# w_out with tokens stationary and 512 columns moving, its sum kept by tokens

## The chip, the cores and the metric

The kernel runs on one core of a Trainium2 chip. The metric is the device time of one execution in microseconds (us). The core has a tensor engine (PE, with the weight loads shown apart as PEld), a vector engine (DVE), a scalar engine (ACT), a general engine (POOL) and a queue engine (SP). Each works off its own instructions in order and waits for the others by semaphores. Here SP issues the weight loads.

## The reference

One layer of a backbone is computed for 128 context tokens and 256 latent tokens (384 in all), with D = 2048 features. What matters is the middle of the layer:

```
def trunk_layer(x, mod, p, ...):
    shift1, scale1, gate1, shift2, scale2, gate2 = jnp.split(mod[:, None, :], 6, axis=-1)
    h = rmsnorm(x, p['norm1']) * (1.0 + scale1) + shift1
    y, kv, st = token_mixers(h, p, ...)          # ends with  y @ p['w_out']
    x = x + gate1 * y
    h = rmsnorm(x, p['norm2']) * (1.0 + scale2) + shift2
    x = x + gate2 * conv_ffn(h, p['w_up'], ..., p['w_down'])
    return x, kv, st
```

`mod` is silu(c) @ w_mod + b_mod: six sections of 2048 columns, with one row of conditioning for the context tokens and one for the latent ones. All is float32.

## The kernel before

**Weights.** All weights stream through SBUF once, in chunks of 128 x 1024 values (512 KB). A `Chunk` is loaded by SP into one of six `raw` buffers, in the order of the list `chunks`, up to five chunks ahead (`LD`). A weight chunk is split in two halves (`do_split`): ACT casts to `hi` (L358), DVE subtracts to get `lo` (L359), each with five buffers. Every product is three matmuls: hi x hi, hi x lo, lo x hi. Two forms exist. `add_wstat` holds 128 x 128 weights in PE and moves 384 token columns (L368 to L370; 386 in w_up, which appends two shift columns); its result lies by features. `add_xstat` holds 128 tokens and moves up to 512 weight columns (L425 to L427); its result lies by tokens, in three of the four banks of `mm_bank`.

**Order.** `chunks` is a list written at trace time, in which `mark(f)` puts code to run at that place. `defer(n, f)` puts `f` off by n half chunks, `settle` runs all that is put off, `pump` steps side work (attention, mLSTM, loads) after each half chunk. The engines' own order comes out of a scheduler that takes the instructions by priority (their order in the code) as it expects them to be ready. The buffers of a tag are handed out in code order.

**Late modulation.** The modulation for the first norm is computed by PE. The other columns of w_mod are done by DVE: `by_dve` is a list of 128 chunks, for 16 blocks of 512 columns, 8 chunks each, in the order 8, 16, 12 (group 0), 9, 17, 13 (group 1), 10, 18, 14, 11, 19, 15, and 20, 21, 22, 23 (group 4). Blocks 8 to 11 are gate 1, 12 to 15 shift 2, 16 to 19 scale 2, 20 to 23 gate 2. `late_mod` adds one chunk into `lacc` (a tag with one buffer) with four DVE instructions (L263, L265). After a block's eighth chunk, `late_sum` sums over partitions on PE (L290, 4 half chunks later), and then `late_out` transposes the block into features (L299), or, for gate 2, `late_row` adds the bias on DVE (L280) and writes a row to DRAM from POOL (L283).

`spread(main, share)` takes a stage's chunks and puts a `by_dve` chunk behind them whenever the shares add up to one. `finish_late(b)` puts all that is left of groups up to b at its place. The shares (`dens`) are 0.25, 0.25, 0.75 and 0.8 for the stages before w_out, 0.5 in w_out and in w_up.

**The stages around the change.** `phase_out(i)`, i from 0 to 7, multiplies by 256 columns of w_out with weights stationary. `load_x1` has fetched x by tokens and transposed it into features (L923); `evac_out` adds gate 1 times the product (L940), squares (L933, L935) and, half a chunk later, `scaled` writes the second input `hh` and its rest (L961, L962). `second_scale` sums the squares over partitions by two matmuls with ones (L971, L972). Then come eleven groups of w_up (`add_up`); from the third on, w_down follows every second group in four blocks of 512 columns (`add_down`), tokens stationary. While the first groups of w_up run, `to_tokens` transposes the sum back to tokens (L1025), to which `gated` adds gate 2 times the product (L1039, L1041). Gate 2 comes as a row from DRAM (`add_rows`), spread over all partitions, in a chunk of its own ahead of a block's last chunk.

Of the kernel before, what the change touches and what calls it, by code (L numbers as in the profile page):

```python
# [7 lines left out]
F32 = mybir.dt.float32  # L8
# [6 lines left out]
P = 128  # L15
# [20 lines left out]
def hybrid_step(  # L36
# [212 lines left out]

    late_acc = {}  # L250

# [17 lines left out]

    gate2 = drp.tile([4, 2 * 512], F32, name="gate2", tag="gate2")  # L270

    def late_row(blk, ev):
        b = blk % 4
        br = sp.tile([P, P], F32, name=nm("brow"), tag="ko")
        G.memset(br, 0.0)
        for i in range(4):
            c0 = 512 * blk + 128 * i
            G.dma_start(out=br[32 * i:32 * i + 1], in_=b_mod[0, c0:c0 + 128].rearrange("(o d) -> o d", o=1))
        for j in range(2):
            V.tensor_tensor(ev[:, 128 * j:128 * j + 128], ev[:, 128 * j:128 * j + 128], br, ALU.add)  # L280
        row = gate2[b:b + 1].rearrange("o (j i c) -> o i j c", j=2, i=4)
        for i in range(4):
            G.dma_start(out=row[:, i], in_=ev[32 * i:32 * i + 1].rearrange("p (j c) -> p j c", j=2))  # L283

    def late_sum(blk):
        acc = late_acc.pop(blk)
        ps = sd_bank()
        for i in range(4):
            for j in range(2):
                T.matmul(ps[32 * i:32 * i + 32, 128 * j:128 * j + 128], lhsT=ones[:, 0:32], rhs=acc[:, j, 128 * i:128 * i + 128],  # L290
                         start=True, stop=True, tile_position=(0, 32 * i))
        ev = sp.tile([P, 256], F32, name=nm("lev"), tag="ropa", bufs=3)
        A.copy(ev, ps[:, 0:256])
        defer(3, lambda: (late_row if blk // 4 == 5 else late_out)(blk, ev))

# [37 lines left out]
    class Chunk:  # L333
        def __init__(self, src, shape, mm, split=True, by_rows=True):
            self.src, self.shape, self.mm, self.split, self.by_rows = src, shape, mm, split, by_rows
            self.raw, self.parts = None, []

        def load(self):
            k, ncol = self.shape
            self.raw = rawp.tile([P, CK], F32, name=nm("raw"), tag="raw")  # L340
            self.v = self.raw[:, :k * ncol].rearrange("p (k c) -> p k c", k=k)
            S.dma_start(out=self.v, in_=self.src)
# [558 lines left out]

    x1 = [None] * KT
    sqacc = const([P, NTOK], "sqacc")

    def load_x1():

        got = {}

        def fetch_x(i):
            a, b = XP[i]  # L910
            for t in range(3):
                got[i, t] = xp.tile([P, NX], F32, name=nm("xa"), tag=f"xl{3 * (i % 5) + t}")
                G.dma_start(out=got[i, t][:, :P * (b - a)], in_=xsrc[t][:, P * a:P * b])

        for i in range(5):
            fetch_x(i)
            yield
        for n in range(KT):
            if n == 4:
                fetch_x(5)  # L920
            ps = sd_bank()
            for t in range(3):
                T.transpose(ps[:, 128 * t:128 * t + 128], got[n // 3, t][:, 128 * (n % 3):128 * (n % 3) + 128], ident)  # L923
            if n % 4 == 0:
                x1g = xp.tile([P, 4, NTOK], F32, name=f"x1_{n}", tag=f"xg{n // 4}")
            x1[n] = x1g[:, n % 4]
            A.copy(x1[n], ps[:, :NTOK])
            yield

    def square_sum(n):  # L930

        q = sqacc if n == 0 else sp.tile([P, NTOK], F32, name=nm("sq"), tag="pT", bufs=3)
        A.activation(q, x1[n][:, :NTOK], AF.Square)  # L933
        if 0 < n < KT - 1:
            V.tensor_tensor(sqacc, sqacc, q, ALU.add)  # L935
        return q

    def residual(n, ps, sec):
        for j, (a, b) in enumerate(SEGS):
            V.scalar_tensor_tensor(x1[n][:, a:b], ps[:, a:b], mod[:, sec, n, j:j + 1], x1[n][:, a:b], ALU.mult, ALU.add)  # L940

    def evac_out(n, ps):
        residual(n, ps, 2)
        q = square_sum(n)
        defer(1, lambda: scaled(n))
        if n == KT - 3:

            A.activation(epsc[:, 1:2], sqacc[:, 0:1], AF.Ln, bias=epsc[:, 0:1])
        if n == KT - 1:
            second_scale(q)  # L950

# [3 lines left out]

    def scaled(n):
        h = xp.tile([P, NX], R32, name=f"hh{n}", tag=f"xl{n}")
        l = slot("hl", R32)[:, :NX]
        x2[n] = (h, l)
        for j, (a, b) in enumerate(SEGS):  # L960
            A.activation(h[:, a:b], x1[n][:, a:b], AF.Copy, scale=sc_[:, 1, n, j:j + 1])  # L961
            V.scalar_tensor_tensor(l[:, a:b], x1[n][:, a:b], sc_[:, 1, n, j:j + 1], h[:, a:b].bitcast(F32),  # L962
                                   ALU.mult, ALU.subtract)
        A.copy(h[:, NTOK:NX], mod[:, 3, n])
        V.tensor_tensor(l[:, NTOK:NX], mod[:, 3, n], h[:, NTOK:NX].bitcast(F32), ALU.subtract)

    rtok = {}

    def second_scale(q):
        ps = sd_bank()  # L970
        T.matmul(ps[:, :NTOK], lhsT=ones, rhs=sqacc, start=True, stop=False)  # L971
        T.matmul(ps[:, :NTOK], lhsT=ones, rhs=q, start=False, stop=True)  # L972
        v = sp.tile([P, 2, NTOK], F32, name="rv", tag="E", bufs=2)
        t = sp.tile([P, 2, NTOK], F32, name="rt", tag="E", bufs=2)[:, 0]
        r = rtok["r"] = slot("rtok")[:, :NX]
        V.memset(r[:, NTOK:NX], 1.0)
        A.activation(v[:, 1], ps[:, :NTOK], AF.Ln, bias=epsc[:, 0:1], scale=1.0 / D)
        V.tensor_scalar(v[:, 0], ps[:, :NTOK], 1.0 / D, EPS, ALU.mult, ALU.add)
        A.activation(r[:, :NTOK], v[:, 1], AF.Exp, scale=-0.5)
        V.tensor_tensor(t, r[:, :NTOK], r[:, :NTOK], ALU.mult)  # L980
        V.scalar_tensor_tensor(t, t, -0.5, v[:, 0], ALU.mult, ALU.mult)
        V.scalar_tensor_tensor(r[:, :NTOK], t, 1.5, r[:, :NTOK], ALU.add, ALU.mult)

# [30 lines left out]

    x1t = [None] * 4

    def to_tokens():
        for b in range(4):  # L1020
            two = s2p.tile([P, 2, 512], F32, name=nm("x1s"), tag="sc")
            banks = [two[:, 0], two[:, 1], sd_bank()]
            for i in range(4):
                for t in range(3):
                    T.transpose(banks[t][:, 128 * i:128 * i + 128], x1[4 * b + i][:, 128 * t:128 * t + 128], ident)  # L1025
                yield
            x1t[b] = xp.tile([P, 3, 512], F32, name=f"x1t{b}", tag=f"xg{b}")
            for t in range(3):
                A.copy(x1t[b][:, t], banks[t])
            yield  # L1030

    def add_rows(src, use):

        ch = Chunk(src.to_broadcast([P, CK]).rearrange("p (k c) -> p k c", k=2), (2, 512), use, split=False)
        return ch

    def gated(t, b, c0, n, ps, gate):

        V.tensor_tensor(ps, ps, gate[:, min(t, 1), c0:c0 + n], ALU.mult)  # L1039
        x = x1t[b][:, t, c0:c0 + n]  # L1040
        V.tensor_tensor(x, x, ps, ALU.add)  # L1041

    def add_down(s_, b):
# [3 lines left out]
                  lambda t, ps: gated(t, b, 0, 512, ps, g2["v"]),  # L1047
                  add_rows(gate2[b:b + 1], lambda ch: g2.update(v=ch.v)))

# [38 lines left out]
    def last_tokens(t):  # L1088
        ssq = sp.tile([P, 5], F32, name=nm("ssqf"), tag="sm")
        at = 0  # L1090
        for b, (c0, c1) in enumerate(BL):
# [12 lines left out]
            while at < 5 and 512 * SQ[at][0] + SQ[at][2] <= c1:  # L1104
                q, a, e = SQ[at]
                junk = sp.tile([P, 2, 512], F32, name=nm("junk"), tag="lacc", bufs=1)[:, 0]
                A.activation(junk[:, 0:e - a], x1t[q][:, t, a:e], AF.Square, accum_out=ssq[:, at:at + 1])
                at += 1
# [113 lines left out]

    def phase_out(i):
        add_wstat(w_out[0], KT, 256 * i, lambda k: ys[k], lambda j, ps: evac_out(2 * i + j, ps))

# [7 lines left out]

    def drain():
        while side:
            pump()

    def settle():
# [5 lines left out]
    finish_late(0)  # L1244
    for i in range(8):
        if i % 2 == 0:
            mark(settle)
        spread(taken(phase_out, i), dens[4])
        finish_late(min(3, i // 2 + 1))

# [6 lines left out]
    for g in range(ngr):  # L1257
        if g == 0:
            mark(lambda: side.append(to_tokens()))
        spread(taken(add_up, g), dens[5])  # L1260
        if g == 2:

            finish_late(4)
            mark(settle)
        if g == 2:
            mark(drain)
        if g >= 2 and g % 2 == 0:
# [6 lines left out]
    for b in range(4):  # L1274
        chunks.append(add_rows(gate2[b:b + 1], lambda ch, b=b: fin["g"].update({b: ch.v})))
        if b % 2:
# [95 lines left out]
```

## Time and profile before

| | |
|---|---|
| median of 3 runs | 2288.24 us (2286.62 to 2288.36) |
| the profiled execution | 2288.0 us |
| its span, first to last instruction | 2286.2 us |
| mean granted clock of PE | 0.999 |
| DVE, busy in the span | 1637.4 us |
| ACT, busy in the span | 1028.0 us |
| POOL, busy in the span | 133.0 us |

A row of a group reads: line, engine, operation, output <- inputs, shapes, count | busy time, mean ns of one | idle time of the engine before, and who ended it. A row of the timeline reads: start, duration, engine, line, operation, shapes, count. Times in the timeline are us from the span's start. Matmuls overlap one another, so their durations add up to more than their engine's time.

### The profile page before, as it was taken

The page shows a single profiled execution, that of the slowest core. Times are in us where ns is not written, and L with a number is a line of the kernel's source. Part 1 is how long each engine was busy: PE and PEld are TensorE (multiplying, and loading weights), DVE is VectorE, ACT ScalarE, POOL GpSimd, SP SyncE. Part 2 cuts the span into 40 slices and gives each one's busy share as a digit, 9 for nine tenths or more (in the row PEclk, how much of TensorE's full clock was granted, in tenths as well). Part 3 has the DMA queues.
Part 4 walks back from the last instruction along what each step waited for, and adds up shares of the span by engine and source line. Part 5 has one row for each costly group of instructions (what it writes and reads, how often), then busy time and mean ns, then how long its engine had stood idle before and what let it go on. Part 6 is the DMA issues. An engine that isn't in the chain of part 4 may idle for free.

```text
span 2286.2 us, 35489 instructions
## 1 busy us (share of the span) xinstructions
PE 2247.7 (98%) x13060; PEld 2096.7 (92%) x13060; DVE 1637.4 (72%) x3419; ACT 1028.0 (45%) x2128; POOL 133.0 (6%) x231
## 2 busy tenths in 40 slices
PE   6999999999999999999999999999999999999998
PEld 5888997899999999999999998998999899889987
DVE  5777777767888989878878895555555556555576
ACT  5232355666555433344454542444345345434541
POOL 1000222211110100010000000000000000000000
PEclk9999999999999999999999999999999999999999
DMA  8787644445555667776645555444433444443462
GB/s 269 251 247 243 188 135 124 131 136 148 171 173 171 177 204 234 226 249 189 189 150 179 179 194 157 129 125 134 155 121 124 153 136 123 131 155 122 137 211 84
DMA packets 306990, 386.13 MB, mean 169 GB/s; under 512 B 16709, under 2 KB 231221, under 8 KB 306817
## 3 DMA queue, kind: packets, MB, share of 16 engines
q1 hardware_dynamic: 301168, 375.24, 53.4%
q0 software_dynamic: 4784, 7.06, 1.1%
q8 instruction: 102, 1.67, 0.3%
q10 hardware_dynamic: 864, 1.57, 0.2%
q14 instruction: 72, 0.58, 0.1%
HBM read 379.08 MB, written 4.74 MB: 168 GB/s over the span
## 4 chain that ended last, share of the span: by engine, by line
PE 92%; DMA 3%; DVE 3%; ACT 1%; issue 1%; SPq 0%; POOL 0%; DVEq 0%; ACTq 0%; POOLq 0%
PE mm L368 22%; PE mm L369 22%; PE mm L370 22%; PE mm L425 6%; PE mm L427 6%; PE mm L426 6%; DMA raw<-in_w_mod_dram 1%; PE mb L227 1%; DMA raw<-in_w_in_dram 1%; DVE lo L359 1%; DVE lacc L265 1%; PE mm L1097 1%; PE mm L1096 1%; PE mm L1098 1%; PE sd L826 1%
## 5 line engine op out<-in xcount | busy, mean ns | idle before, releaser
L358 ACT CAST hi<-raw 128x512 fp32r<-128x512 f32 x960 | 590.6, 620 | 984.3 <-PE mm L369 590.9
L359 DVE TENSOR_TENSOR lo<-raw,hi 128x512 fp32r<-128x512 f32 x960 | 659.0, 692 | 477.4 <-ACT hi L358 473.7
L368 PE MATMUL mm<-hh,hi 128*128 128x386 f32 x1408 | 480.1, 341 | 0.0
L369 PE MATMUL mm<-hl,hi 128*128 128x386 f32 x1408 | 479.6, 341 | 0.0
L370 PE MATMUL mm<-hh,lo 128*128 128x386 f32 x1408 | 478.8, 340 | 0.0
L368 PE MATMUL mm<-xg,hi 128*128 128x384 f32 x1024 | 354.4, 347 | 2.2 <-ACT hi L358 1.4
L265 DVE SCALAR_TENSOR_TENSOR lacc<-raw,scT,lacc 128x512 f32<-128x512 f32 x480 | 342.5, 747 | 17.9 <-DMA raw<-in_w_mod_dram 17.7
L369 PE MATMUL mm<-xl,hi 128*128 128x384 f32 x1024 | 345.8, 338 | 0.0
L370 PE MATMUL mm<-xg,lo 128*128 128x384 f32 x1024 | 345.2, 337 | 0.0
L368 PEld LDWEIGHTS mm<-hh,hi 128*128 128x128 f32 x1408 | 267.9, 190 | 1.1 <-ACT hi L358 0.4
L370 PEld LDWEIGHTS mm<-hh,lo 128*128 128x128 f32 x1408 | 266.9, 190 | 0.0
L369 PEld LDWEIGHTS mm<-hl,hi 128*128 128x128 f32 x1408 | 266.5, 189 | 0.3
L368 PEld LDWEIGHTS mm<-xg,hi 128*128 128x128 f32 x1024 | 192.3, 188 | 21.2 <-issue 14.0
L369 PEld LDWEIGHTS mm<-xl,hi 128*128 128x128 f32 x1024 | 192.5, 188 | 1.5 <-issue 1.4
L370 PEld LDWEIGHTS mm<-xg,lo 128*128 128x128 f32 x1024 | 192.3, 188 | 0.4 <-issue 0.2
L427 PE MATMUL mm<-hi,gl 128*128 128x512 f32 x480 | 189.2, 394 | 0.0
L426 PE MATMUL mm<-lo,gh 128*128 128x512 f32 x480 | 189.2, 394 | 0.0
L425 PE MATMUL mm<-hi,gh 128*128 128x512 f32 x480 | 186.8, 394 | 0.0
L425 PEld LDWEIGHTS mm<-hi,gh 128*128 128x128 f32 x480 | 90.2, 188 | 21.3 <-DVE x1t L1041 0.2
L427 PEld LDWEIGHTS mm<-hi,gl 128*128 128x128 f32 x480 | 90.2, 188 | 21.0
L426 PEld LDWEIGHTS mm<-lo,gh 128*128 128x128 f32 x480 | 90.2, 188 | 20.9
L503 DVE TENSOR_TENSOR qk<-qk,mm 128x384 f32<-128x384 f32 x160 | 85.7, 549 | 21.4 <-PE mm L370 20.9
(350 smaller groups left out, 3065.3 us busy)
## 6 DMA issues: line engine op xcount, KB each, us to landing
raw<-in_w_mod_dram SPq DMA_DIRECT2D x192, 512.0 KB, 4.4
raw<-in_w_up_dram SPq DMA_DIRECT2D x176, 512.0 KB, 3.6
raw<-in_w_in_dram SPq DMA_DIRECT2D x160, 512.0 KB, 4.6
raw<-in_w_down_dram SPq DMA_DIRECT2D x80, 512.0 KB, 3.9
raw<-in_w_out_dram SPq DMA_DIRECT2D x32, 512.0 KB, 4.4
raw<-gate SPq DMA_DIRECT2D x24, 512.0 KB, 4.6
raw<-in_w_pb_dram SPq DMA_DIRECT2D x16, 512.0 KB, 3.9
raw<-in_w_pa_dram SPq DMA_DIRECT2D x16, 512.0 KB, 4.5
```

What stands on the lines that cost most here:

```text
L227: T.matmul(self.bank[32 * q:32 * q + 32, 0:self.width], lhsT=scT[:, k, 2 - 2 * i:34 - 2 * i], rhs=w[:, kk], start=i == 0 and k < 4, stop=i ...
L265: V.scalar_tensor_tensor(acc[:, j], w[:, kk], col, acc[:, j], ALU.mult, ALU.add)
L358: A.copy(h, v)
L359: V.tensor_tensor(l, v, h.bitcast(F32), ALU.subtract)
L368: T.matmul(ps, lhsT=wh, rhs=xh, start=first, stop=False)
L369: T.matmul(ps, lhsT=wh, rhs=xl, start=False, stop=False)
L370: T.matmul(ps, lhsT=wl, rhs=xh, start=False, stop=last)
L425: T.matmul(ps, lhsT=xh_[:, ts_], rhs=h[:, kk], start=k == ks[0], stop=False)
L426: T.matmul(ps, lhsT=xh_[:, ts_], rhs=l[:, kk], start=False, stop=False)
L427: T.matmul(ps, lhsT=xl_[:, ts_], rhs=h[:, kk], start=False, stop=k == ks[-1])
L503: V.tensor_tensor(dst[h][:, :NTOK], dst[h][:, :NTOK], ps, ALU.add)
L826: T.matmul(pv_[:, d], lhsT=E[:, d, t], rhs=vt[:, t], start=True, stop=not (t == 2 - d))
```

## The change

w_out is multiplied in four blocks of 512 columns with tokens stationary. x is loaded by tokens straight into the tiles that hold the sum, and isn't transposed any more; the product is multiplied by a row of gate 1 and added there. `scaled` transposes the sum, four feature tiles for each block, and writes the second input from PSUM. The squares are summed by tokens on ACT; `second_scale` takes the root with small DVE steps and spreads the three columns over partitions with three matmuls (ones times a diagonal). Gate 1 goes to DRAM as rows, like gate 2, so blocks 8 to 11 use `late_row`. `to_tokens` and its `drain` are gone. In each block of w_out, `by_dve` chunks are spread among the first five of nine chunks; `finish_late(b)` and a `settle` stand behind these.

```diff
-    gate2 = drp.tile([4, 2 * 512], F32, name="gate2", tag="gate2")
+    gates = {sec: [drp.tile([1, 2 * 512], F32, name=f"gate{sec}_{b}", tag=f"gate{sec}_{b}") for b in range(4)]
+             for sec in (2, 5)}
...
-        defer(3, lambda: (late_row if blk // 4 == 5 else late_out)(blk, ev))
+        defer(3, lambda: (late_row if blk // 4 in (2, 5) else late_out)(blk, ev))
...
     def load_x1():
+        for b in range(4):
+            x1t[b] = xp.tile([P, 3, 512], F32, name=f"x1t{b}", tag=f"xg{b}")
             for t in range(3):
-                T.transpose(ps[:, 128 * t:128 * t + 128], got[n // 3, t][:, 128 * (n % 3):128 * (n % 3) + 128], ident)
+                G.dma_start(out=x1t[b][:, t], in_=xsrc[t][:, 512 * b:512 * b + 512])
...
+    def evac_out(b, t, ps, gate):
+        gated(t, b, 0, 512, ps, gate)
+        if t == 2:
+            for i in range(4):
+                defer(i + 1, lambda i=i: scaled(4 * b + i))
...
     def scaled(n):
+        b, i = n // 4, n % 4
+        ps = sd_bank()
+        for t in range(3):
+            T.transpose(ps[:, 128 * t:128 * t + 128], x1t[b][:, t, 128 * i:128 * i + 128], ident)
...
+            A.activation(h[:, a:e], ps[:, a:e], AF.Copy, scale=sc_[:, 1, n, j:j + 1])
+            V.scalar_tensor_tensor(l[:, a:e], ps[:, a:e], sc_[:, 1, n, j:j + 1], h[:, a:e].bitcast(F32),
                                    ALU.mult, ALU.subtract)
...
+        if i == 3:
+            for t in range(3):
+                junk = sp.tile([P, 2, NTOK], F32, name=nm("junk"), tag="E", bufs=2).rearrange("p a b -> p (a b)")
+                A.activation(junk[:, 0:512], x1t[b][:, t], AF.Square, accum_out=ssq2[:, t, b:b + 1])
+            if b == 3:
+                second_scale()
...
+    def second_scale():
+        tot = sp.tile([P, 3], F32, name="tot2", tag="ssqa")
+        V.tensor_reduce(tot, ssq2, AX.X, ALU.add)
+        rs = rms_scale(tot, 3, D)
...
+        for t in range(3):
+            dg = sp.tile([P, P], F32, name=nm("dg"), tag="sqj")
+            V.tensor_scalar(dg, ident, rs[:, t:t + 1], None, ALU.mult)
+            T.matmul(ps[:, 128 * t:128 * t + 128], lhsT=ones, rhs=dg, start=True, stop=True)
+        A.copy(r[:, :NTOK], ps[:, :NTOK])
...
-    def phase_out(i):
-        add_wstat(w_out[0], KT, 256 * i, lambda k: ys[k], lambda j, ps: evac_out(2 * i + j, ps))
+    def phase_out(b):
+        g1 = {}
+        add_xstat(w_out[0], range(KT), 512 * b, 512, lambda k: ys[k], lambda t, ps: evac_out(b, t, ps, g1["v"]),
+                  add_rows(gates[2][b], lambda ch: g1.update(v=ch.v), 8 + b))
...
-    for i in range(8):
-        if i % 2 == 0:
-            mark(settle)
-        spread(taken(phase_out, i), dens[4])
-        finish_late(min(3, i // 2 + 1))
+    for b in range(4):
+        mark(settle)
+        main = taken(phase_out, b)
+        spread(main[:5], dens[4])
+        finish_late(b)
+        mark(settle)
+        chunks.extend(main[5:])
...
     for g in range(ngr):
-        if g == 0:
-            mark(lambda: side.append(to_tokens()))
         spread(taken(add_up, g), dens[5])
         if g == 2:
 
             finish_late(4)
             mark(settle)
-        if g == 2:
-            mark(drain)
```

More of the change, by code (lines that the diff above doesn't have):

```diff
@@ L248, in finish @@
                                 ALU.add)
-    late_acc = {}
+    late_acc, written = {}, set()
     def late_mod(raw, blk, kg):
@@ L280, in late_row @@
             V.tensor_tensor(ev[:, 128 * j:128 * j + 128], ev[:, 128 * j:128 * j + 128], br, ALU.add)
-        row = gate2[b:b + 1].rearrange("o (j i c) -> o i j c", j=2, i=4)
+        row = gates[blk // 4][b].rearrange("o (j i c) -> o i j c", j=2, i=4)
+        written.add(blk)
         for i in range(4):
@@ L335, in __init__ @@
             self.src, self.shape, self.mm, self.split, self.by_rows = src, shape, mm, split, by_rows
-            self.raw, self.parts = None, []
+            self.raw, self.parts, self.need = None, [], None
         def load(self):
+            assert self.need is None or self.need in written
             k, ncol = self.shape
@@ L900, in evac_pa @@
         defer(1, lambda: V.tensor_tensor(yl, s, y.bitcast(F32), ALU.subtract))
-    x1 = [None] * KT
-    sqacc = const([P, NTOK], "sqacc")
+    x1t = [None] * 4
     def load_x1():
-        got = {}
-        def fetch_x(i):
-            a, b = XP[i]
+        for b in range(4):
+            x1t[b] = xp.tile([P, 3, 512], F32, name=f"x1t{b}", tag=f"xg{b}")
             for t in range(3):
[L912 to L916, printed above, removed]
+                G.dma_start(out=x1t[b][:, t], in_=xsrc[t][:, 512 * b:512 * b + 512])
@@ L917, in load_x1 @@
             yield
[L918 to L950, printed above, removed]
+    def add_rows(src, use, need=None):
+        ch = Chunk(src.to_broadcast([P, CK]).rearrange("p (k c) -> p k c", k=2), (2, 512), use, split=False)
+        ch.need = need
+        return ch
@@ new lines, in gated, with square @@
+    def gated(t, b, c0, n, ps, gate):
+        V.tensor_tensor(ps, ps, gate[:, min(t, 1), c0:c0 + n], ALU.mult)
+        x = x1t[b][:, t, c0:c0 + n]
+        V.tensor_tensor(x, x, ps, ALU.add)
+    ssq2 = const([P, 3, 4], "ssq2")
+    def square(x, acc):
+        junk = sp.tile([P, 2, 512], F32, name=nm("junk"), tag="lacc", bufs=1)[:, 0]
+        A.activation(junk[:, 0:x.shape[-1]], x, AF.Square, accum_out=acc)
+    def evac_out(b, t, ps, gate):
[3 more added lines that the diff above has]
+                defer(i + 1, lambda i=i: scaled(4 * b + i))
@@ L959, in scaled @@
         x2[n] = (h, l)
-        for j, (a, b) in enumerate(SEGS):
-            A.activation(h[:, a:b], x1[n][:, a:b], AF.Copy, scale=sc_[:, 1, n, j:j + 1])
-            V.scalar_tensor_tensor(l[:, a:b], x1[n][:, a:b], sc_[:, 1, n, j:j + 1], h[:, a:b].bitcast(F32),
+        for j, (a, e) in enumerate(SEGS):
+            A.activation(h[:, a:e], ps[:, a:e], AF.Copy, scale=sc_[:, 1, n, j:j + 1])
+            V.scalar_tensor_tensor(l[:, a:e], ps[:, a:e], sc_[:, 1, n, j:j + 1], h[:, a:e].bitcast(F32),
                                    ALU.mult, ALU.subtract)
@@ L965, in scaled @@
         V.tensor_tensor(l[:, NTOK:NX], mod[:, 3, n], h[:, NTOK:NX].bitcast(F32), ALU.subtract)
-    rtok = {}
[L969 to L974, printed above, removed]
+        if i == 3:
[4 more added lines that the diff above has]
+                second_scale()
+    rtok = {}
+    def second_scale():
+        tot = sp.tile([P, 3], F32, name="tot2", tag="ssqa")
+        V.tensor_reduce(tot, ssq2, AX.X, ALU.add)
+        rs = rms_scale(tot, 3, D)
         r = rtok["r"] = slot("rtok")[:, :NX]
         V.memset(r[:, NTOK:NX], 1.0)
[L977 to L982, printed above, removed]
+        ps = sd_bank()
+        for t in range(3):
[3 more added lines that the diff above has]
+        A.copy(r[:, :NTOK], ps[:, :NTOK])
     za, gs = {}, {}
@@ L1013, in evac_b @@
         defer(1, product)
[L1017 to L1041, printed above, removed]
     def add_down(s_, b):
@@ L1047, in add_down @@
                   lambda t, ps: gated(t, b, 0, 512, ps, g2["v"]),
-                  add_rows(gate2[b:b + 1], lambda ch: g2.update(v=ch.v)))
+                  add_rows(gates[5][b], lambda ch: g2.update(v=ch.v), 20 + b))
     KL = range(NF - 4, NF)
@@ L1105, in last_tokens @@
                 q, a, e = SQ[at]
-                junk = sp.tile([P, 2, 512], F32, name=nm("junk"), tag="lacc", bufs=1)[:, 0]
-                A.activation(junk[:, 0:e - a], x1t[q][:, t, a:e], AF.Square, accum_out=ssq[:, at:at + 1])
+                square(x1t[q][:, t, a:e], ssq[:, at:at + 1])
                 at += 1
@@ L1232, in hybrid_step @@
     dens = (.25, .25, .75, .8, .5, .5)
-    def drain():
-        while side:
-            pump()
     def settle():
@@ L1274, in hybrid_step @@
     for b in range(4):
-        chunks.append(add_rows(gate2[b:b + 1], lambda ch, b=b: fin["g"].update({b: ch.v})))
+        chunks.append(add_rows(gates[5][b], lambda ch, b=b: fin["g"].update({b: ch.v})))
         if b % 2:
```

## The prediction

> **What bounds the kernel now.** I read the page first, then the windows, then single stretches of the timeline.
>
> ```profile
> span 2286.2 us, 35489 instructions
> ...
> PE 2247.7 (98%) x13060; PEld 2096.7 (92%) x13060; DVE 1637.4 (72%) x3419; ACT 1028.0 (45%) x2128; POOL 133.0 (6%) x231
> ...
> PE 92%; DMA 3%; DVE 3%; ACT 1%; issue 1%; SPq 0%; POOL 0%; DVEq 0%; ACTq 0%; POOLq 0%
> ```
>
> The chain that ended last lies on PE for 92% of the span: the time is what PE streams plus the little it waits. So the change is worth the PE work that it takes away, less each wait it puts before PE. Next, by stage (columns: stretch, its length, busy time and instructions of PE, PEld, DVE, ACT, POOL, then granted clock, DMA share, GB/s). The w_out stage runs from 1002 to 1144, and behind it the first three groups of w_up to 1359; 1564 to 1628 is a stretch of w_down, which already has tokens stationary and 512 columns moving.
>
> ```profile
> 1002.00:1144.00 142.00, 142.00 (x854) 140.58 (x853) 119.41 (x236) 65.44 (x144) 1.58 (x3) 1.00 0.62 193
> 1046.00:1098.00 52.00, 52.00 (x298) 52.00 (x297) 40.88 (x90) 23.35 (x49) 0.00 (x0) 1.00 0.55 172
> 1180.00:1350.00 170.00, 170.00 (x985) 168.92 (x984) 148.88 (x285) 86.81 (x166) 8.38 (x19) 1.00 0.59 184
> 1564.00:1628.00 64.00, 64.00 (x278) 51.90 (x277) 36.27 (x61) 21.62 (x38) 0.00 (x0) 1.00 0.50 155
> ```
>
> PE is never idle in the stage that is changed. DVE is busy for 119.41 of 142 there and for 148.88 of 170 (88%) in w_up up to 1350: it has little to spare, and that decides this case.
>
> **The matmuls themselves.** One matmul lasts some 0.34 us, but the next starts before it ends, so I price them by the rate. 384 columns: 52.00 / 298 = 0.1745 us. 512 columns: 64.00 / 278 = 0.2302 us. Before, w_out takes 8 parts x 2 column tiles x 16 k x 3 = 768 matmuls of 384 columns, 134.0 us; after, 4 blocks x 3 token tiles x 16 k x 3 = 576 of 512 columns, 132.6 us. That is -1.4 us: the columns streamed are the same. The Trainium skill, "TensorE: Matmul & The Clock Gate", section "Back-to-back issue gap", puts the gap at N / 2.4 + 2.5 ns; by that the 192 matmuls saved would be worth 0.5 us, and the rows here give more.
>
> **Transposes.** Before, the kernel transposes x into features (48, L923) and the sum back into tokens (48, L1025); after, only the sum (48, in `scaled`). Three of them, set between matmuls, cost:
>
> ```profile
> 1008.74 0.34 PE L370 MATMUL mm<-yh,lo 128*128 128x384 f32 x1
> 1008.92 0.49 PE L923 MATMUL sd<-cst,xa 128*128 128x128 f32 x3
> 1009.16 0.43 PE L368 MATMUL mm<-yh,hi 128*128 128x384 f32 x1
> 1009.42 0.34 PE L369 MATMUL mm<-yl,hi 128*128 128x384 f32 x1
> ```
>
> From 1008.74 to 1009.42 are 0.68 us for two matmuls (0.35) and three transposes: 0.33 us per three. The 16 triples of L1025 go: -5.3 us. Those of L923 give way to as many in `scaled`: 0. Gate 1 becomes rows, so `late_out` falls away for 4 blocks, each two transposes, two thirds of such a triple, 0.22 us: -0.9 us.
>
> **The second norm** is now summed by token on ACT and spread over partitions by three small products. Before:
>
> ```profile
> 1145.69 0.34 PE L370 MATMUL mm<-hh,lo 128*128 128x386 f32 x1
> 1146.31 0.91 PE L971 MATMUL sd<-sqacc,ones 128*128 128x384 f32 x2 [0.28 <-DVE sqacc L935]
> 1147.06 0.81 PE L972 MATMUL sd<-sq,ones 128*128 128x384 f32 x2
> 1147.40 0.63 PE L368 MATMUL mm<-hh,hi 128*128 128x386 f32 x1
> 1147.87 0.34 PE L369 MATMUL mm<-hl,hi 128*128 128x386 f32 x1
> ```
>
> 2.18 us less two matmuls: 1.8 us. The new one is a third as wide: three products of two passes, at the 0.11 us of a transpose each, 0.7 us. Net -1.1 us. These rows show a second thing. In the code L971 stands ahead of all w_up matmuls, yet nine of them ran first: the instruction order on an engine is planned by expected readiness, and the plan missed here by about 0.44 us (1146.31 against 1145.69 + 0.18). The new transposes hang on DVE's evacuation in the same way, once a block: 4 x 0.44 = +1.8 us. The ends are 0 (w_down has like block ends in its 64 busy us) and, in code order, some 5 us a block: three evacuations of two 0.6 us steps, and 1.4 for the turns of the two banks; that end is a rival below.
>
> **Side work.** The 12 evacuations cost DVE two steps each, 1.2 us by the 0.61 of a `lo` of the same width (1359.82 to 1360.43, below), in place of 32 residuals and 14 additions; in w_out DVE gets lighter, so nothing is charged. Four gate rows of 512 KB on SP's queue are hidden at a DMA share of 0.62. Four more `late_row` put a memset and 8 DMA issues each on POOL, at its mean of 0.58 us (133.0 / 231); behind them queue rope steps of the attention and mask steps of the mLSTM. POOL is 6% busy, so I take 0; the other end is one `late_row` in the attention's way, 5.2 us. One cost is less visible: the squares write to a tile of tag E (two buffers), and both hold the last two y tiles until the last w_out matmul:
>
> ```profile
> L370 PE MATMUL mm<-yhl,lo x32: 336/338/343, 1019.3 to 1144.1; 128*128 128x384 f32 x32
> ...
> 2262.56 0.63 ACT L1107 ACTIVATE junk<-x1t 128x512 f32<-128x512 f32 x1 [0.60 <-DVE x1t L1041]
> 2263.10 0.19 ACT L1107 ACTIVATION_READ_ACCUMULATOR junk<-x1t 128x1 f32 x1
> ```
>
> So nine squares of 0.54 + 0.19 us, 6.6 us, come on ACT at the start of w_up, ahead of later `hi` casts. Cover: five half chunks cast ahead, 12 matmuls or 2.1 us of PE each. I charge +1.0 us, between 0 and 6.6.
>
> **What is moved, and the wait it makes.** The late modulation (`by_dve`, 128 chunks: 16 column blocks of 8) is strewn among the weight chunks. A stage of n weight chunks takes n times its share: 16 x 0.25, 33 x 0.25, 48 x 0.75 and 48 x 0.8, whole ones, make 4 + 8 + 36 + 38 = 86 before w_out in both kernels. Before, each of the 8 w_out parts takes 2 (16 in all), the three w_up groups 8 each, and 2 are left for `finish_late(4)` ahead of w_down. After, only the first five chunks of each of four blocks are spread: 2 each, and 2 more by `finish_late(3)`: 10. The groups take 24 again, so 8 chunks, 120 to 127, stand in one row ahead of w_down: the whole of column block 23. Each needs DVE:
>
> ```profile
> L265 DVE SCALAR_TENSOR_TENSOR lacc<-raw,scT,lacc 128x512 f32<-128x512 f32 x480 | 342.5, 747 | 17.9 <-DMA raw<-in_w_mod_dram 17.7
> ...
> 1313.18 0.67 PE L290 MATMUL sd<-lacc,ones 128*32 128x128 f32 x16
> ...
> 1314.38 0.88 DVE L263 TENSOR_SCALAR lacc<-raw,scT 128x512 f32<-128x512 f32 x2
> ...
> 1351.80 2.07 DVE L265 SCALAR_TENSOR_TENSOR lacc<-raw,scT,lacc 128x512 f32<-128x512 f32 x3
> ...
> 1358.83 0.66 PE L290 MATMUL sd<-lacc,ones 128*32 128x128 f32 x16
> 1359.42 0.50 PE L425 MATMUL mm<-hi,gh 128*128 128x512 f32 x1
> ...
> 1359.82 0.69 DVE L359 TENSOR_TENSOR lo<-raw,hi 128x512 fp32r<-128x512 f32 x1 [0.32 <-ACT hi L358]
> 1360.43 0.74 DVE L994 SCALAR_TENSOR_TENSOR z<-u,cw,z 128x127 f32<-128x127 f32 x2
> 1361.09 0.74 DVE L995 SCALAR_TENSOR_TENSOR z<-u,cw,z 128x127 f32<-128x127 f32 x2
> ```
>
> Three in a row take 2.07 us, the last of them 0.747, so one starts every 0.66 us; two L263 take 0.88, about 0.40 from one to the next. The first chunk is 2 x 0.40 + 2 x 0.66 = 2.1 us, seven more are 2.65 each: 20.7 us. They can't begin early. Their accumulator has one buffer, and block 22's has to be summed by PE (L290) first; the two rows around 1314 show this wait, 1.2 us from L290 to L263. In the new order block 22's last chunk stands behind the last matmul chunk of the group, so its L290 comes only with the `settle` after the row. So at the end of w_up's third group, call it T, PE runs L290 and has nothing left: the weights of w_down queue behind the eight chunks for the six raw buffers, and their `lo` stands behind them on DVE. Before, w_down began 0.6 us after T (1358.83 to 1359.42). After: 1.2 + 20.7, the four convolution steps of the last tile 1.3 (0.66 for two), two products and two short `lev` sums about as much, 1.3, one `lo` 0.6, signals 0.4: T + 25.5. That is +24.9 us of idle PE. Low end 20 (the sum comes a chunk and a half earlier), high end 28. An idle PE also loses its clock:
>
> ```profile
> 2275.00:2279.00 4.00, 1.09 (x10) 0.95 (x9) 2.96 (x13) 1.17 (x6) 0.00 (x0) 1.00 0.00 0
> 2279.00:2283.00 4.00, 0.00 (x0) 0.00 (x0) 3.37 (x8) 0.00 (x0) 0.00 (x0) 0.57 0.40 151
> 2283.00:2286.00 3.00, 0.00 (x0) 0.00 (x0) 0.00 (x0) 0.00 (x0) 0.00 (x0) 0.50 0.43 149
> ```
>
> PE's last matmul ends 1.09 us into the first row; 0.57 is a fall to 0.50 at 2279.56, some 3.5 us later. No row shows the way back. If it takes as long, as I estimate, 3.5 us at half speed lose +1.7 us; the ends are 0 and twice that. The Trainium skill speaks against the change here, in "TensorE: Matmul & The Clock Gate", "Part 1: The HAM clock gate": an idle window of about 3.4 us halves the clock, and about 3.4 us of work restore it; by that the term would be 1.7 us, and the trace bears out the fall only.
>
> **Sum.** -1.4 - 5.3 - 0.9 - 1.1 + 1.8 + 1.0 + 24.9 + 1.7 = +20.7 us. The profiled execution took 2288.0 us for a span of 2286.2; the median of the runs is 2288.24, so I use 2288.0: 2308.7 us.
>
> **Rivals.** (a) The weights of w_down are not held up: the planned order lets their loads and `lo` pass the eight chunks. DVE is idle for 43% of w_down (36.27 of 64 busy), so 20.7 us would fit within its first three blocks; the last two terms vanish, and the sum is -5.9: 2282 us, faster. For it speaks that engine orders are planned; against it that loads follow code order through a ring of six buffers, so w_down's first load waits for the third of the eight. It decides if that load is issued before block 22 is summed. (b) The row is worked off in part before T, because PE sums block 22 some chunks early. If 10 to 18 us of it are hidden: 2291 to 2299. Against it: DVE idles 12% (21 us of 170), so this takes 80 us of lead and more, and L290 stands just where the code puts it. (c) Evacuation and transposes stay in code order: 5 us at four block ends, 20 less the 1.8: 2327. Against it: the nine matmuls ahead of L971. (d) The change does nothing in sum (the rows after w_out spread as before, gains eaten by waits): 2286 to 2291.
>
> **Chances.** Forecast, 2300 to 2320: 0.75. (a) 0.08, (b) 0.06, (c) 0.08, (d) 0.03. The range 2298 to 2322 takes in the ends of the squares, the clock and the wait, and the edges of (b) and (c). About 0.2% (4.6 us) is what a measurement can tell from no change: faster 0.09, same 0.03, slower 0.88.
>
> **What would show it.** Right: one PE gap of 24 to 26 us between the last w_up matmul of the third group and the first of w_down, DVE full of L265 in it, clock 0.5 at its end, w_out's stage some 1 us shorter, the next w_up group as long as before. Wrong: w_down's first `lo` among the L265, or the gap missing; gaps of several us at each block end of w_out; or a PE wait for `hi` just after w_out, which would be the squares.

## The result and the profile after

The changed kernel takes 2312.53 us (median of 4 runs, 2311.3 to 2315.85) against 2288.3 for the kernel before (4 runs, 2286.62 to 2288.78): a ratio of 1.0109, 95% interval 1.0097 to 1.0122. It is slower by 24 us. The forecast was 2308.7 with a range of 2298 to 2322. The profiled execution of after took 2311.3 us, with a span of 2309.6. Its page says (span, busy time by engine, shares of the chain that ended last, and the granted clock in 40 slices):

```profile
span 2309.6 us, 34978 instructions
...
PE 2245.2 (97%) x12814; PEld 2065.4 (89%) x12814; DVE 1637.9 (71%) x3413; ACT 1015.9 (44%) x2104; POOL 146.5 (6%) x261
...
PEclk9999999999999999999999979999999999999999
...
PE 89%; DVE 4%; DMA 3%; ACT 1%; issue 1%; POOL 0%; SPq 0%; DVEq 0%; ACTq 0%; POOLq 0%
```

PE has 246 matmuls fewer and is the last engine for 89% of the chain where it was 92%. One slice of the clock line, 1328 to 1386 us, reads 7: something happens once, not all along.

The windows of after place it (w_out; the first three groups of w_up; from there to the end of w_down's first four blocks), with the same three stretches of before under them:

```profile
1002.10:1144.15 142.05, 140.97 (x650) 111.98 (x648) 97.76 (x180) 51.30 (x101) 0.00 (x0) 1.00 0.58 184
1144.15:1353.50 209.35, 209.28 (x1214) 207.31 (x1216) 174.42 (x350) 106.94 (x214) 8.38 (x18) 1.00 0.59 179
1353.50:1449.37 95.87, 72.00 (x320) 56.93 (x310) 62.08 (x105) 25.95 (x45) 4.01 (x8) 0.86 0.51 154
```

```profile
1002.30:1144.30 142.00, 142.00 (x854) 140.58 (x854) 119.41 (x237) 65.47 (x145) 1.58 (x3) 1.00 0.62 192
1144.30:1358.80 214.50, 214.22 (x1253) 211.32 (x1251) 179.67 (x342) 110.47 (x211) 10.37 (x22) 1.00 0.57 178
1358.80:1426.28 67.48, 67.48 (x305) 54.65 (x305) 38.56 (x67) 23.22 (x41) 2.00 (x4) 1.00 0.48 155
```

w_out takes as long as before, w_up some 5 us less, and w_down's first four blocks 28 us more, with PE busy for 72 of 95.87 us and a mean clock of 0.86. Taken exactly, from the first w_out matmul to T (the L290 of before, L292 of after, behind the third w_up group): 1002.02 to 1353.22, 351.20 us, against 1002.30 to 1358.83, 356.53. That is -5.3. From T to the next w_up group: 96.15 against 67.45, +28.7. Ahead of w_out the two differ by 0.3, behind w_down's first blocks by 0.3. The sum is the 23.4 us between the spans.

The hole itself, in the timeline of after (in brackets: idle time before the row, and who ended it), first PE, then DVE, then SP's loads:

```profile
1353.22 0.66 PE L292 MATMUL sd<-lacc,ones 128*32 128x128 f32 x16
1368.65 1.65 PE L428 MATMUL mm<-hi,gh 128*128 128x512 f32 x3 [14.76 <-ACT hi L361]
1376.90 1.67 PE L292 MATMUL sd<-lacc,ones 128*32 128x128 f32 x16 [6.60 <-DVE lacc L265]
1381.08 0.80 PE L429 MATMUL mm<-lo,gh 128*128 128x512 f32 x1 [2.50 <-DVE lo L362]
1381.67 0.63 PE L430 MATMUL mm<-hi,gl 128*128 128x512 f32 x1
...
1385.51 0.42 PE L429 MATMUL mm<-lo,gh 128*128 128x512 f32 x1
```

```profile
1352.26 0.56 DVE L985 TENSOR_TENSOR u<-mm,rtok 128x386 f32<-128x386 f32 x1 [8.39 <-PE mm L373]
...
1353.99 0.48 DVE L263 TENSOR_SCALAR lacc<-raw,scT 128x512 f32<-128x512 f32 x1
...
1357.46 19.96 DVE L265 SCALAR_TENSOR_TENSOR lacc<-raw,scT,lacc 128x512 f32<-128x512 f32 x30
1377.34 1.02 DVE L1005 TENSOR_TENSOR z<-z,z 128x384 f32<-128x384 f32 x2
...
1380.34 3.09 DVE L362 TENSOR_TENSOR lo<-raw,hi 128x512 fp32r<-128x512 f32 x5
```

```profile
1327.89 34.02 SPq L345 DMA_DIRECT2D raw<-in_w_mod_dram  x9
1364.20 5.67 SPq L345 DMA_DIRECT2D raw<-in_w_down_dram  x3
```

Read them together. PE finishes the third group and sums block 22 at 1353.22. Only then may DVE write block 23's first value, at 1353.99, because the accumulator has one buffer. DVE had idled 8.39 us just before, up to 1352.26. All eight chunks follow, thirty L265 in 19.96 us, 0.665 from one to the next, and w_down's first `lo` comes at 1380.34 behind them. SP issued the last late loads and then, 11 us after T, w_down's first. The row names ACT's `hi` as the end of PE's first wait (the cast waits for that load), and DVE's `lo` as the end of the last. Three hi x hi matmuls run early at 1368.65; the next weight product in PE's order needs `lo`.

The clock, in two windows inside it and one behind:

```profile
1370.00:1381.00 11.00, 1.97 (x17) 0.82 (x16) 10.77 (x22) 3.05 (x6) 1.70 (x4) 0.50 0.65 192
1381.00:1386.00 5.00, 4.92 (x12) 3.88 (x13) 3.12 (x6) 0.62 (x1) 2.31 (x5) 0.55 0.57 162
1386.00:1449.00 63.00, 63.00 (x273) 50.99 (x272) 31.41 (x49) 18.61 (x30) 0.00 (x0) 1.00 0.50 155
```

In the hole it is 0.50. The eleven matmul starts from 1381.08 to 1385.51 are 0.44 us apart on average, those behind them 0.231 (63 / 273).

### The profile page after: what moved, and what is told of

Read it like the earlier page. It is cut to its first block, busy times and chain, and to the rows that moved or that the text cites. A ratio compares the mean times of both kernels' runs of the same rounds, so it can differ in the third digit from the quotient of the medians.

```text
span 2309.6 us, 34978 instructions
## 1 busy us (share of the span) xinstructions
PE 2245.2 (97%) x12814; PEld 2065.4 (89%) x12814; DVE 1637.9 (71%) x3413; ACT 1015.9 (44%) x2104; POOL 146.5 (6%) x261
## 4 chain that ended last, share of the span: by engine, by line
PE 89%; DVE 4%; DMA 3%; ACT 1%; issue 1%; POOL 0%; SPq 0%; DVEq 0%; ACTq 0%; POOLq 0%
PE mm L371 20%; PE mm L372 20%; PE mm L373 20%; PE mm L428 7%; PE mm L429 7%; PE mm L430 7%; DMA raw<-in_w_mod_dram 2%; DVE lacc L265 1%; PE mb L227 1%; DVE lo L362 1%; PE mm L1066 1%; PE mm L1065 1%; PE mm L1064 1%; PE sd L829 0%; DMA raw<-in_w_in_dram 0%
## 5 line engine op out<-in xcount | busy, mean ns | idle before, releaser
L265 DVE SCALAR_TENSOR_TENSOR lacc<-raw,scT,lacc 128x512 f32<-128x512 f32 x480 | 342.0, 747 | 23.0 <-DMA raw<-in_w_mod_dram 22.8
```

What stands on the lines that cost most here:

```text
L265: V.scalar_tensor_tensor(acc[:, j], w[:, kk], col, acc[:, j], ALU.mult, ALU.add)
```

## The experiments

The theory from this reading: the row of eight late chunks ahead of w_down costs all that was lost and more. It is DVE's time, 2.65 us a chunk, and none of it is hidden, because block 23 can't begin before T and DVE works in order. The rest of the change gains a few us. Rivals: the loss lies in the new w_out itself (its block ends, its second input), so that it stays when the row is gone; or the row waits for its loads, not for DVE.

**The row taken away.** 16 late chunks in w_out as before, so that 2 are left ahead of w_down (diffs are against the changed kernel, unless the text says otherwise):

```diff
-        spread(main[:5], dens[4])
+        spread(main[:5], .9)
```

> The changed kernel with four late chunks per w_out block in place of two (16 in w_out, so two are left in front of w_down, as before the change). Theory (the row of eight late chunks is the loss): the PE gap in front of w_down goes, 28.7 us of the changed kernel's 2312.5 go with it, 2283 to 2285 us, some 5 us under the kernel before. Rival (the new form of w_out, its evacuations and gate rows, costs the time): no more than a few us change, 2308 or more.

Measured: 2284.17 us (2281.81 to 2287.37, 11 runs), ratio 0.9984 (0.9975 to 0.9993). PE at the seam, and who kept it waiting before the transposes of the sum:

```profile
1355.27 0.66 PE L292 MATMUL sd<-lacc,ones 128*32 128x128 f32 x16
1355.86 0.50 PE L428 MATMUL mm<-hi,gh 128*128 128x512 f32 x1
1356.20 0.39 PE L429 MATMUL mm<-lo,gh 128*128 128x512 f32 x1
```

```profile
L948 PE MATMUL sd<-cst,x1t x48: 270/272/328, 1038.2 to 1153.2; 128*128 128x128 f32 x48
its engine sat idle before it (us, times) until:
  DVE x1t L926: 2.4, 2
```

The hole is gone and with it 28.4 us, as the theory said; the loss doesn't lie in w_out. A little comes back there: six more late chunks on DVE make PE wait 2.4 us for the evacuation L926, where the same view of after reads 0.7.

**The row put into the kernel before** (the diff is against that kernel), 10 late chunks in w_out and none of the rest of the change:

```diff
-        spread(taken(phase_out, i), dens[4])
+        spread(taken(phase_out, i), dens[4] if i < 5 else 0)
```

> The kernel before the change, with late chunks in the first five w_out parts only (10 in place of 16), so that the same eight are left in one row in front of w_down. Nothing else differs from the kernel before. Theory: the same gap of 27 to 28 us and 2 us at half clock appear without any of the change: 2315 to 2318 us. Rival (the new form of w_out is needed for the loss): 2288.

Measured: 2317.24 us (2315.6 to 2319.34, 4 runs), ratio 1.0132 (1.0118 to 1.0146). PE in front of w_down:

```profile
1357.59 0.67 PE L290 MATMUL sd<-lacc,ones 128*32 128x128 f32 x16
1373.13 1.65 PE L425 MATMUL mm<-hi,gh 128*128 128x512 f32 x3 [14.88 <-ACT hi L358]
1381.27 1.67 PE L290 MATMUL sd<-lacc,ones 128*32 128x128 f32 x16 [6.50 <-DVE lacc L265]
1385.45 0.79 PE L426 MATMUL mm<-lo,gh 128*128 128x512 f32 x1 [2.51 <-DVE lo L359]
```

The same hole stands in a kernel whose w_out is the old one: 14.88, 6.50 and 2.51 us of waiting against 14.76, 6.60 and 2.50. So it costs 29.7 us here (2317.2 less 2287.5) and 28.4 in the new kernel, and the rest of the change is worth -3.4 us without the row (e1 against before) and -4.7 with it (after against this one). Of the 1.3 us between these two, some 0.8 is the clock: here the slow starts last from 1385.45 to 1391.57, which loses 2.9 us, against 2.1 in after.

**DVE or the loads.** Block 23 leaves out two of the four DVE instructions of each of its chunks; the loads stay:

```diff
-        for kk in range(2):
+        for kk in range(1 if blk == 23 else 2):
```

> After, but column block 23 (the row) adds only the first of each chunk's two row tiles: two of the four DVE instructions of each of its eight chunks are left out, so gate 2's last 512 columns lack half of their sum; all loads stay. Theory, DVE's time sets the gap: eight chunks lose two starts of 0.66 us each, 10.6 us, so the w_down stage ends about 85.5 us behind the third group instead of 96.2, and the median is 2312.5 - 10.6 = 2301.9 us (2300 to 2304). Rival, the row is paced by its loads: 512 KB at the 192 GB/s that the row of after moved are 2.7 us a chunk, no less than DVE's 2.65, so halving DVE's work changes less than 3 us: 2309 or more.

Measured: 2298.45 us (2297.9 to 2299.69, 4 runs), ratio 1.0045 (1.003 to 1.006). That is 14.1 below after, more than the 10.6 expected and outside the 2300 to 2304. The row on DVE:

```profile
1358.19 9.36 DVE L265 SCALAR_TENSOR_TENSOR lacc<-raw,scT,lacc 128x512 f32<-128x512 f32 x14
1367.46 1.02 DVE L1005 TENSOR_TENSOR z<-z,z 128x384 f32<-128x384 f32 x2
...
1368.81 0.69 DVE L362 TENSOR_TENSOR lo<-raw,hi 128x512 fp32r<-128x512 f32 x1
```

Fourteen in 9.36 us is still 0.67 apart: with half the work the loads keep up, so DVE paced the row, and the rival on loads falls. The stretch from T to the fourth w_up group is 83.2 us (96.2 in after), 13.0 less rather than 10.6. Three things make up the difference: `lo` comes 1.35 us behind the last L265 here and 3.0 in after, since `gl` now stands behind it (-1.7); the slow starts of w_down's `lo` products last from 1370.19 to 1371.91 only (-1.3); and PE now sums block 23 between `lo` and its matmul (+0.6).

**The accumulator.** Block 23 gets a buffer of its own, so that it needn't wait for T:

```diff
-            late_acc[blk] = sp.tile([P, 2, 512], F32, name=nm("lacc"), tag="lacc", bufs=1)
+            late_acc[blk] = sp.tile([P, 2, 512], F32, name=nm("lacc"), tag="E" if blk == 23 else "lacc", bufs=2 if blk == 23 else 1)
```

> The changed kernel, with column block 23 adding up in a buffer of its own (tag E), so that its eight chunks need not wait for PE to sum block 22. Theory (the wait fixes the start, DVE's 20.7 us fix the length): DVE was idle for 10.3 of the 18.4 us ahead of the row, so about that much of it is done early; a gap of some 16 us stays: 2300 to 2303 us. Rival A (the single buffer is the whole loss): 2284. Rival B (DVE's amount alone, the buffer doesn't matter): 2312.

Measured: 2300.59 us (2299.7 to 2301.64, 4 runs), ratio 1.0059 (1.0045 to 1.0072). DVE:

```profile
1342.42 8.69 DVE L265 SCALAR_TENSOR_TENSOR lacc<-raw,scT,lacc 128x512 f32<-128x512 f32 x13
...
1357.87 7.37 DVE L265 SCALAR_TENSOR_TENSOR lacc<-raw,scT,lacc 128x512 f32<-128x512 f32 x11
...
1368.16 3.09 DVE L362 TENSOR_TENSOR lo<-raw,hi 128x512 fp32r<-128x512 f32 x5
```

T is at 1351.61 here. DVE writes block 23's first value at 1334.80, 17 us ahead of it instead of 0.8 behind, and 12 us of the loss go. The rest stays: up to T DVE has other work as well, half of the row comes behind it, and the `lo` of w_down behind that. The single buffer sets when the row starts, and DVE's time sets what it costs from there.

**Four chunks left** instead of eight or two:

```diff
-        spread(main[:5], dens[4])
+        spread(main[:5], .9 if b < 2 else .7)
```

> The changed kernel with 4, 4, 3 and 3 late chunks in the four w_out blocks (14 in place of 10), so that four are left in one row in front of w_down, and block 22 ends eight matmul chunks earlier. Theory (DVE's backlog decides, with some 8 us of cover from chunks split ahead): most of the row runs before w_up ends; a gap of 2 to 6 us is left: 2286 to 2291 us. Rival (each chunk in the row costs its 2.65 us and the clock's 2 us come in any case): four rows 10.6 + 2 + 2284: 2296 or more.

Measured: 2295.28 us (2294.33 to 2296.24, 5 runs), ratio 1.0033 (1.0021 to 1.0046): above the 2286 to 2291 that the theory gave and under the rival's 2296, so neither held. DVE's windows before T, and PE after it:

```profile
1300.00:1320.00 20.00, 20.00 (x114) 20.00 (x113) 12.88 (x25) 9.74 (x18) 0.00 (x0) 1.00 0.59 184
1320.00:1335.00 15.00, 15.00 (x98) 14.55 (x97) 13.88 (x30) 7.43 (x16) 1.40 (x3) 1.00 0.40 124
1335.00:1356.00 21.00, 21.00 (x120) 21.00 (x119) 20.50 (x36) 9.58 (x18) 0.62 (x2) 1.00 0.69 214
```

```profile
1356.43 0.86 PE L428 MATMUL mm<-hi,gh 128*128 128x512 f32 x3
1363.79 1.67 PE L292 MATMUL sd<-lacc,ones 128*32 128x128 f32 x16 [6.50 <-DVE lacc L265]
1365.90 0.80 PE L429 MATMUL mm<-lo,gh 128*128 128x512 f32 x1 [0.44 <-DVE lo L362]
```

I had counted on idle time of DVE ahead of T. There is some, 7 us up to 1320, but from there DVE is busy for 34.4 of 36 us (34.7 in e1). The two chunks more than in e1 find no room. They cost more than their own 5.3 us, since the order turns. In e1 the first `lo` of w_down is made before T (at 1353.72 at the latest, where T is 1355.27). Here the first comes at 1365.16, behind the last six L265 (4.0 us) and, as in after, behind the convolution of two tiles and the products (3.6), which in e1 come after it. The slow matmul starts, from 1365.90 to 1369.06, add 1.5. The median is 11.1 us above e1's.

**None left:** 20 chunks in w_out (the diff is that of e1 with `1.`).

> The changed kernel with five late chunks behind the first five chunks of each w_out block (20), so that none is left in front of w_down and w_up's third group gets fewer. Theory: no gap in front of w_down, but DVE is fuller in w_out, where PE waits for its sums at each block's end (1.2 to 1.5 us at two ends with four late chunks): 2283 to 2287 us, like e1 or a little slower. Rival (fewer late chunks in w_up help, since DVE is the fuller there): under 2282.

Measured: 2288.17 us (2284.12 to 2291.55, 10 runs), ratio 1.0002 (0.9993 to 1.0011): above the 2283 to 2287 expected, and not under 2282 as the rival said. What PE waits for before the transposes of the sum:

```profile
L948 PE MATMUL sd<-cst,x1t x48: 270/272/331, 1039.4 to 1155.4; 128*128 128x128 f32 x48
its engine sat idle before it (us, times) until:
  DVE x1t L926: 3.3, 3
```

The stage from the first w_out to the first w_up matmul takes 145.6 us, against 142.3 in e1. The four chunks more in w_out are two fewer in w_up and none instead of two ahead of w_down, where e1 has no hole either. From w_up to w_down 2.5 us are won (209.35 against 211.88). In w_out 3.3 are lost: PE idles 2.1 us more there (3.8 against 1.7), and works 1.2 us more, with one more block's sum in this stage. That is 0.8 us in sum; the profiled executions are 2.1 us apart and the medians 4.0, so most of the difference isn't accounted for.

**Strewn in w_down** instead of in front of it, one behind each of its first chunks:

```diff
-            finish_late(4)
...
+                if by_dve:
+                    chunks.append(by_dve.pop(0)[1])
```

> The changed kernel, with the last eight late chunks strewn among the first w_down chunks, one behind each, in place of in a row ahead of them. The same DVE work, at the same point of the program. Theory (it is a matter of the queue order, not of DVE's amount: DVE idles 43% of w_down): no PE gap over 1 us, 2283 to 2286 us. Rival (DVE has no room for them there either): a gap of 10 us or more remains, 2295 or more.

Measured: 2288.41 us (2285.07 to 2290.12, 11 runs), ratio 1.0004 (0.9995 to 1.0013): 2.4 above the end of what was expected. A window of its w_down:

```profile
1366.00:1380.00 14.00, 10.61 (x42) 7.27 (x41) 14.00 (x23) 3.65 (x7) 0.00 (x0) 1.00 0.71 234
```

DVE is busy for all of the 14 us, and PE idles for 3.4, with two waits over the 1 us that the theory allowed (1.1 and 1.6). DVE's 43% of idle time in w_down is a mean. With a late chunk behind each, a w_down chunk asks for 2.65 us, two `lo` of 0.6 and a quarter of a block's evacuation (six steps of 0.6), 4.8 us of DVE; PE needs 18 x 0.231 = 4.2 for it. The median is still 24 us below that of the row.

**The price of a transpose triple**, the largest gain in the forecast. In the e1 version, `scaled` makes its three transposes twice:

```diff
-        for t in range(3):
+        for t in (0, 1, 2, 0, 1, 2):
```

> The version with 16 late chunks in w_out (spread 0.9), but scaled() makes its three transposes twice into the same bank: 48 more transposes. Theory, a triple costs PE 0.33 us, as read from before: +5.3 us to that version's 2284.2, 2289.5 us (2288 to 2291). Rival, PE waits at the block ends for DVE anyway (3.5 us of such waits in that version), and the transposes lie beside these waits: under +2 us, 2286 or less.

Measured: 2287.7 us (2286.73 to 2289.93, 10 runs), ratio 0.9999 (0.9989 to 1.0008), so +3.5 us on e1, between the two.

```profile
L948 PE MATMUL sd<-cst,x1t x96: 270/273/329, 1037.0 to 1155.9; 128*128 128x128 f32 x96
its engine sat idle before it (us, times) until:
  DVE x1t L926: 1.3, 4
```

From the first w_out to the first w_down matmul the profiled runs are 3.9 us apart (358.15 and 354.22). The waits before these transposes are 1.1 us smaller (1.3 against 2.4): 3.9 + 1.1 = 5.0 for 16 triples, 0.31 each. PE's busy time in these stretches, 356.48 against 351.00 us, gives 5.5, or 0.34 each. So the price of 0.33 fits, as far as one trace of each can show it. That PE's waits for DVE cover a part of it fits the smaller waits, but wasn't tried by itself.

**Two more placements.** Both let what is put off at the end of a w_out block run on into the next one. The first is e1 without the `settle` at the head of blocks 1 to 3:

```diff
-        mark(settle)
+        if b == 0:
+            mark(settle)
```

> As e1 (16 late chunks in w_out), and the transposes of a block aren't all placed at the start of the next block (settle there only ahead of the first), but one every half chunk as evac_out puts them off. Theory: PE's waits at the block ends come from transposes that are planned ahead of matmuls which could run; put off, they cost nothing: e1 less 1 to 3 us, 2281 to 2283. Rival (the wait is for DVE itself and only moves): 2284 as e1.

Measured: 2284.41 us (2280.71 to 2287.79, 11 runs), ratio 0.9985 (0.9976 to 0.9994): the same as e1, as the rival said, and not 1 to 3 us less.

The second spreads the late chunks over all nine chunks of a block, without the `settle` in the middle either:

```diff
-        mark(settle)
+        if b == 0:
+            mark(settle)
         main = taken(phase_out, b)
-        spread(main[:5], dens[4])
+        spread(main, dens[4])
         finish_late(b)
-        mark(settle)
-        chunks.extend(main[5:])
```

> As e7, with the four late chunks of a w_out block spread over all nine chunks in place of the first five, and no settle in the middle. Theory: DVE is less crowded at each block's start, where it has the sums of the block before: as e7 or up to 1 us less, 2280 to 2283. Rival (late chunks beside the last chunks of a block delay the sums): 1 to 3 us slower than e7.

Measured: 2283.57 us (2281.0 to 2286.25, 11 runs), ratio 0.9981 (0.9973 to 0.9990). It has the lowest median, 29 us under the change as made and 4 under the kernel before, and lies 0.6 above the 2280 to 2283 expected. The ratios of e1 and e7 lie within its interval, so between the three nothing is decided.

## Why the prediction was right, and where its sizes were off

The mechanism was the one forecast: one hole between the third w_up group and w_down (PE idles 23.9 us, in three pieces), DVE full of L265 in it, the clock at 0.50 at its end. e1 takes it out, e3 makes it in the old kernel, e9 shows that DVE paces it, and e2 shows that the one accumulator sets its start.

- **The row, predicted 24.9 + 1.7, measured 28.7.** The eight chunks were sized well: 0.77 us from L292 to L263 (1.2 forecast), 0.665 us a step. What was undersized is the work behind and among them, "the four convolution steps of the last tile 1.3 ... two products and two short `lev` sums about as much". The convolution of two tiles, not of one, came after T: eight steps, 2.6 us. The two products, four `lev` sums and two `gl` took 3.0 us, from 1377.34 to 1380.34. The first lo matmul starts at T + 27.9 where T + 25.5 was said. Less the 0.7 us of three matmuls that ran early and before's 0.6, and with the clock's 2.1: 28.7.
- **The clock, predicted 1.7, measured 2.1.** Ten steps from start to start in 4.43 us are 2.1 more than ten of 0.231. The 1.7 rested on an estimate that the way back takes as long as the fall; other runs show anything from 3.2 to 6.1 us (last section), so that it came out so near is luck.
- **Up to T.** Stream, triples, norm, waits and squares were to give -1.4 - 5.3 - 1.1 + 1.8 + 1.0 = -5.0; measured -5.3. The triples are borne out by e10; the stream and the norm were not tried one by one. The waits show in w_out's window, PE idle 1.1 us of 142.05. Counted from one matmul's start to the next, four waits of 0.3 to 0.5 us in w_out and a fifth in w_up make 2.0. But 0.5 of it, up to 1003.89, is of a kind I hadn't named: a block takes three banks at once, and the last two tiles of the stage before still hold two. **The squares' +1.0 was wrong**: PE is busy for 209.28 of 209.35 us of w_up, so they held nothing up. With waits of 2.0 and no charge for the squares, the stream, the triples and the norm together gave 7.3 us and not 7.8. So errors of 1.0 one way and 0.7 the other nearly cancel, and the closeness of -5.0 and -5.3 is in part luck. Traces of the same code scatter besides: the stretch up to T takes 351.1 us in e2, 351.5 in e4 and 353.3 in e9 (there the wait up to 1003.88 is 1.8 us), and 357.0 in e3 against 356.5 in before.
- **`late_out`, predicted -0.9.** Ahead of w_out the two kernels differ by 0.3 us, too little to tell from what such a stretch scatters by: in the profiled executions of all the kernels w_out starts between 1000.05 us (e7) and 1003.37 (e8). It stays open.
- **The 1 us that w_out's stage was to lose** wasn't there (142.05 against 142.00): its gain lies in w_up, where `to_tokens` ran.
- **The rivals.** (a) fell by the test that it named: w_down's first load is issued 11 us after T. (b) fell as well, the row was whole behind T; e2 is what it would have looked like. (c) fell: four block-end waits under 0.6 us each in after (under 0.8 in e9), not 5. (d) is nearly what the change is once the row is out: e1 gives -3.4 us.

The forecast is 3.8 us below the median: 2.1 of it is the row with its clock, 0.6 `late_out`, -0.3 the work up to T, 0.3 the stages behind, and 1.2 is how far the profiled execution of after lies under its median.

## What to carry to other kernels

When a change alters how many pieces a stage has, count again the side work that is handed out by pieces: here eight of 128 chunks slid to a seam, and that cost more than six times the 3.4 to 4.7 us that the rest of the change gained. In-order side work is free only up to the engine's idle time in that stretch, not in the mean of the stage; ask at each seam what stands in that engine's queue ahead of the first input of the next stage, and through which single buffer it must pass. Among the placements tried, those with four late chunks in each w_out block were the fastest (e1, e7, e8); how they lie within a block made no difference that could be told. More of them there (e6), or a string of them in w_down (e4), took some 4 us longer.

## What the runs showed of the hardware

The way back of the clock, of which before had no row: in after PE's matmuls start 0.44 us apart for 4.4 us after the hole, then 0.231; the granted clock reads 0.50, 0.55 and 1.00 in the three windows above. The Trainium skill, "TensorE: Matmul & The Clock Gate", section "Part 1: The HAM clock gate", says about 3.4 us of work. The traces here agree with it only in part: counted from the first matmul of the steady stream, the slow starts last 3.2 us in e5 (1365.90 to 1369.06), 4.3 in e9 (1367.58 to 1371.91, which takes in block 23's sum), 4.4 in after, 5.3 in e2 (1368.90 to 1374.18) and 6.1 in e3 (1385.45 to 1391.57). What sets this length was not tried. The waits in e4's window, none over 1.6 us long, left the clock at 1.00.

The versions without the hole scatter more than the kernel before: 11 runs lie within 5.6 us in e1 and 7.1 in e7, 28 runs of before within 4.5. The four runs of after lie within 4.6, too few to compare. Some of it is the stretch ahead of w_out, where the profiled executions differ by up to 3.3 us; another part is the first wait in w_out, 0.5 us in after and 1.8 in e9. What makes them vary was not tried.
